# Gate tiles ahead of the waiting tiles in the DeltaNet layer, and row sums written as full 128x128 products

## The chip, the core and the metric

The kernel runs on one core of a Trainium2 chip. A core has TensorE (PE in the profile; its weight loads are listed apart as PEld), VectorE (DVE), ScalarE (ACT), GpSimd (POOL) and SyncE (SP, whose queue issues the transfers here). The metric is the device time of one execution in microseconds; lower is better.

## The reference, cut to what matters

A trunk of four layers over 272 tokens (16 learned meta tokens and 256 real ones) of width 1024. Every layer is a token mixer and then a SwiGLU network of inner width 2816, each on a normalised copy of the residual and added back to it. The mixers are in turn forgetting attention (FoX, 16 heads of 64), gated linear attention (GLA, 4 heads), gated DeltaNet (8 heads of 128) and FoX again.

```python
for i in range(DEPTH):                       # FoX, GLA, DeltaNet, FoX
    h = h + mixer(rmsnorm(h, norm_mix[i]))
    h = h + swiglu(rmsnorm(h, norm_ffn[i]), w_gate_up[i], w_down[i])

def gdn_mixer(h, ...):                       # the DeltaNet layer
    proj = h @ w_in                          # q, k, v, gate: 1024 columns each; a, beta
    qkv = silu(causal_depthwise_conv(qkv, conv_w))
    q = l2norm(q) * 128 ** -0.5;  k = l2norm(k)
    ...                                      # per chunk and head:
    t_mat = I + strict_lower(kb k^T * decay) # unit lower triangular
    u, w = solve(t_mat, [v beta, kb exp(b)])
    v_new = u - w @ state
    o = (q k^T * decay) @ v_new + (q exp(b)) @ state
    o = rmsnorm(o, o_gain) * silu(gate)
    return o @ w_out
```

FoX normalises q and k per head (a sum of squares over 64 channels), GLA and DeltaNet normalise their outputs per head (256 and 128 channels), and DeltaNet's q and k too. These per-head sums of squares are the row sums of this case.

## The kernel before, in words

**Layout.** Activations are kept transposed: 128 channels on the partitions, 272 tokens along the free axis. A "column tile" is 128 output channels of a projection. Each needs eight input blocks, and each block needs three matmuls of 272 columns, since inputs and weights are split in a high and a low part in a one-pass format (`zh`, `zl` with `wh`, `wl`; `Trunk.block`, where `mm` at L403 is the line that all matmuls carry). These are the dense matmuls. Other matmuls keep plain float32 operands; the trace shows two records for each of them.

**Weights.** Each column tile has one weight unit of 128x1024 (`make_unit`): a transfer of 512 KB on SP's queue, a copy `wh` on ACT, a subtraction `wl` on DVE. Units are made in the order of the column tiles, up to two ahead of the one in use, with three buffers each.

**Order.** The program is written out by one generator-driven planner, `Trunk`, which estimates when each engine is free and emits instructions in that order (`turn`, `step`, `Lane.slot`). Column tiles stand in a list `bg`, first in, first out: at most three are open, and if the tile at the head waits for an event that isn't set, none behind it may start (`step`). Everything else (convolutions, Gram products, the inverse, the solves) is a generator that runs when its inputs are estimated to be there. The planner's estimate of the PE clock counts columns weighted by the rows of the moving operand over 128 (`pe`); it has no price for a change of the used part of the array. The lanes of ACT and DVE put the weight split (`wide`) into the first free slot after its inputs.

**DeltaNet.** `GDN_ORDER` lists the column tiles of its input projection: keys `k`, gates `r`, queries `q`, values `v`. Tiles at place `GDN_FREE` = 19 or later that are not gates wait for `in_ev` (in `gdn`, where `self.dense` is called for the list). `in_ev` is set by `inverse()`: the decays (`decay`), the key norms (`k_done`) and the Gram products (`gram`) lead to 24 lower triangular 96-token blocks, whose 16x16 diagonal blocks are inverted together by a chain of 15 steps on DVE, two instructions each. Then `merge` combines the small inverses by small matmuls, `solve(i)` runs for each head, `wrap` and `out_norm` normalise, and the output projection follows (`finish`). Up to six convolution inputs `xc` are held at a time (`GDN_XC`); queries and values that were projected early wait for `in_ev` with their convolution. A finished gate tile needs one DVE product (`sr` from PSUM times the row scale) and one Silu on ACT (`r_done`), and is not needed before `gated(i)`.

**Row sums.** A sum of squares over the channels of a head is a matmul whose stationary operand is a window of a mostly zero strip (`strip1`, `strip2`) with one or two non-zero columns. The window is 8 columns wide, so the stationary operand is 128x8, and the sum lands in row i of an 8-row output. Four or eight heads are accumulated in one bank. The way back, from 8 rows to 128 partitions, is a matmul of a selector (`sel`, `sel2` through `pick`) with a 64-row tile that holds high and low parts (`rows_tile`, `hilo_rows`): 64 rows of contraction. The norm of the residual uses a 128x128 constant `ones` (`norm_end`).

Of the kernel before, what the change touches and what calls it, by code (L numbers as in the profile page):

```python
# [9 lines left out]
F32R = mybir.dt.float32r  # L10
# [6 lines left out]
DM = 1024  # L17
NM = 16
T = 272
# [8 lines left out]
GLA_GROUP = 8  # L28
# [5 lines left out]
GDN_ORDER = (  # L34
    [("k", i) for i in range(8)]
    + [("r", i) for i in range(5)]
    + [(c, i) for i0 in (0, 4) for c in "qv" for i in range(i0, i0 + 4)]
    + [("r", i) for i in range(5, 8)]
)
KEPT = ("_const_", "_z_", "_wraw_", "_wsp_", "_ps_")  # L40

# [97 lines left out]
def shape_consts():  # L139
    c = Cols()  # L140
    c.add("ident", np.eye(128))
    c.add("ones", np.full((128, 128), 1.0 / DM))
    strip = np.zeros((128, 30))
    strip[:64, 14] = 1.0 / 64
    strip[64:, 15] = 1.0 / 64
    c.add("strip2", strip)
    strip = np.zeros((128, 15))
    strip[:, 7] = 1.0
    c.add("strip1", strip)
    c.add("sel", np.tile(np.eye(32, 16), (4, 1)))  # L150
    return c

# [140 lines left out]
class Trunk:  # L293
# [357 lines left out]
    def norm_end(self):  # L651
        yield self.acc
        p = yield from self.bank()
        self.mm(p[:, :T], self.con("ones"), self.acc)
        self.v.tensor_scalar(self.ms, p[:, :T], EPS, None, ALU.add)
        self.free(p)
        yield from self.rsqrt(self.zp, self.rs, self.ms, rest=True)
        self.set(self.rs_ev)
# [41 lines left out]

        return self.sel[rows, h : h + 1].to_broadcast([rows.stop - rows.start, n])

    def rows_tile(self, pool, name, n=T, rows=64, bufs=None):
        st = pool.tile([128, n], F32R, tag=name, name=name, bufs=bufs)[:rows]
        self.v.tensor_scalar(st, self.con_t[:rows, 0:1].to_broadcast([rows, n]), 0.0, None, ALU.mult)
        return st
# [61 lines left out]
    def fox(self, j, lo, gain):  # L768
        v, s, g = self.v, self.s, self.g
# [8 lines left out]
        with ExitStack() as cx:  # L778
            cp = cx.enter_context(self.tc.tile_pool(name="foxc", bufs=1))
# [38 lines left out]
            GP = FOX_GROUP  # L818

            def qk_done(jp, which):  # L820
                grp, i = jp // GP, 2 * (jp % GP) + which

                def f(p):
                    raw = tp.tile([128, T], F32, tag=f"raw{i}", name="raw", bufs=2)
                    s.activation(raw, p[:, :T], AF.Copy)
                    sq = tp.tile([128, T], F32, tag="sq", name="sq", bufs=3)
                    s.activation(sq, p[:, :T], AF.Square)
                    self.free(p)
                    raws[jp, which] = raw
                    yield sq  # L830
                    if i == 0:
                        ssqs[grp] = yield from self.bank()
                    ssq = ssqs[grp]
                    n = 4 * GP
                    self.mm(ssq[:n, :T], self.con("strip2")[:, 14 - 2 * i : 14 + n - 2 * i], sq, i == 0, i == 2 * GP - 1)
                    if i == 2 * GP - 1:
                        mm = tp.tile([n, T], F32, tag="mm", name="mm")
                        v.scalar_tensor_tensor(mm, ms[:n], EPS, ssq[:n, :T], ALU.mult, ALU.add)
                        self.free(ssq)
                        y = tp.tile([n, T], F32, tag="y", name="y")  # L840
                        yield from self.rsqrt(self.zp, y, mm)
                        ys = self.rows_tile(tp, "ys")
                        self.hilo_rows(ys, y, 0)
                        yield ys
                        for i2 in range(2 * GP):
                            jq = grp * GP + i2 // 2
                            p = yield from self.bank()
                            self.mm(p[:, :T], self.sel2[:, i2], ys)
                            r = raws[jq, i2 % 2]
                            v.scalar_tensor_tensor(r, r, kg if i2 % 2 else qg, p[:, :T], ALU.mult, ALU.mult)  # L850
                            self.free(p)
                            if i2 % 2:
                                self.set(qk_ev[jq], r, raws[jq, 0])
                return f
# [124 lines left out]
    def gla(self, j, lo, gain):  # L979
        v, s, g = self.v, self.s, self.g  # L980
# [3 lines left out]
        with ExitStack() as cx:  # L984
# [3 lines left out]
            cp = cx1.enter_context(self.tc.tile_pool(name="glac", bufs=1))  # L988
# [193 lines left out]
            def out(i):  # L1182
                yield at_ev
                yield v_ev[i]
                hd, grp = i // 2, i // GLA_GROUP
                p = yield from self.bank()
                for i3, (t0, n) in enumerate(TILES):
                    self.mm(p[:, t0:T], vsb[i3][:, i], at[i3][:n, hd, : T - t0], i3 == 0, i3 == 2)
                obs[i] = post[0].tile([128, T], F32, tag="ob", name="ob", bufs=KD)
                s.activation(obs[i], p[:, :T], AF.Copy)  # L1190
                self.set(o_ev[i], obs[i])
                yield from self.hold("sq", 3)
                sq = tp.tile([128, T], F32, tag="sq", name="sq", bufs=3)
                s.activation(sq, p[:, :T], AF.Square)
                self.free(p)
                yield sq
                if banks[grp] is None:
                    banks[grp] = yield from self.bank()
                r = hd % (GLA_GROUP // 2)
                self.mm(banks[grp][:8, :T], self.con("strip1")[:, 7 - r : 15 - r], sq, count2[grp] == 0, count2[grp] == GLA_GROUP - 1)  # L1200
                self.drop("sq")
                count2[grp] += 1
                if count2[grp] == GLA_GROUP:
                    self.set(s_ev[grp])
# [42 lines left out]
    def out_norm(self, new, tp, mm, ob, g_ev, oh_ev, tiles, row):  # L1247

        v = self.v
        y = self.zp.tile([128, T], F32, tag="nsq", name="y", bufs=2)[:8]  # L1250
        yield from self.rsqrt(self.zp, y, mm)
        ys = self.rows_tile(self.zp, "nacc", bufs=2)
        self.hilo_rows(ys, y, 0)
        for i in tiles:
            self.oh[i], self.ol[i] = new("oh"), new("ol")
        self.oh_ready = True
        yield ys
        for i in tiles:
            yield g_ev[i]
            p = yield from self.bank()  # L1260
            self.mm(p[:, :T], self.pick(slice(0, 64), row(i)), ys)
            yield from self.hold("vt", 2)
            og = tp.tile([128, T], F32, tag="vt", name="og")
            v.tensor_mul(og, ob[i], p[:, :T])
            self.free(p)
            self.split(self.oh[i], self.ol[i], og)
            self.drop("vt")
            self.set(oh_ev[i], self.oh[i], self.ol[i])


    def gdn(self, j, lo, gain):
        v, s, g = self.v, self.s, self.g
# [4 lines left out]
        with ExitStack() as cx:  # L1277
# [87 lines left out]
            def row_sum(name, i, sq):  # L1365
                if i % 4 == 0:
                    bank[name] = yield from self.bank()
                self.mm(bank[name][:8, :T], self.con("strip1")[:, 7 - i % 4 : 15 - i % 4], sq, i % 4 == 0, i % 4 == 3)
                self.drop("sq")

            def decay():
# [6 lines left out]
                for i0 in range(0, H, GDN_DECAYS):  # L1378
                    ps = yield from self.bankn(GDN_DECAYS)
                    for i, p in enumerate(ps, i0):  # L1380
                        self.mm(p[:96, 0:T], self.pick(slice(0, 64), i, 96), bs, True, False)
                        self.mm(p[:96, T:448], self.pick(slice(0, 64), i, 96), bs[:, 96:], False, False)
                        self.mm(p[:96, 0:96], eye, dmask[:, 0:96], False, False)
                        self.mm(p[:96, T:448], eye, dmask, False, True)
                    for i, p in enumerate(ps, i0):
# [8 lines left out]
            def k_done(i):  # L1394
                def f(p):
# [12 lines left out]
                    if i == 0:  # L1408
                        bank["k"] = yield from self.bank()
                    for i3, (t0, n) in enumerate(TILES):  # L1410
                        self.mm(bank["k"][:n, 8 * i3 + i : 8 * i3 + i + 1], sq[:, t0 : t0 + n], self.con("strip1")[:, 7:8])
                    self.drop("sq")
                    if i == H - 1:
                        pk = bank["k"]
# [304 lines left out]
    def run(self):  # L1719
        nc, tc = self.nc, self.tc  # L1720
        self.new_pools()
        with ExitStack() as cx:
# [6 lines left out]
            self.par_t = cp.tile([128, self.pcols.n], F32, name="par")  # L1729
            self.con_t = cp.tile([128, self.ccols.n], F32, name="con")  # L1730
            self.sel = cp.tile([128, 16], F32R, name="sel")
            self.sel2 = cp.tile([64, 4, 128], F32R, name="sel2")
            self.next_norm()
            self.nblock = 8 * 3
            self.make_unit()
# [10 lines left out]
            def start():  # L1746
                for k in range(KD):
                    self.norm_z(k, f"g_mix{self.layers[0][0]}")
                for k in range(KD):
                    self.norm_sum(k)  # L1750
                self.v.tensor_copy(self.sel, self.con("sel"))
                pairs = self.con("sel")[:64, 0:8].rearrange("p (i a) -> p i a", a=2)
                self.v.tensor_copy(
                    self.sel2.rearrange("p i (a b) -> p i a b", a=2), pairs[:, :, :, None].to_broadcast([64, 4, 2, 64]))
                yield from self.norm_end()

            self.go(start())
# [47 lines left out]
```

## Time and profile before

| | |
|---|---|
| median of three runs | 1587.0 us (1582.32 to 1587.86) |
| profiled execution, its own time | 1581.87 us |
| its span | 1580.1 us |
| mean granted PE clock | 0.977 |
| PE busy | 1518.4 us (96%) |
| DVE busy | 1097.7 us (69%) |
| ACT busy | 779.7 us (49%) |

The span is the traced stretch; 1.8 us of the execution lie around it. PE records overlap, since matmuls are pipelined: the distance between the starts of two matmuls says what one costs, not its listed duration. The granted clock is 1.00 at full speed and 0.50 at half speed; dense matmuls then start about 0.125 or 0.227 us apart.

### The profile page before, as it was taken

The numbers are of one execution on the slowest core, as the hardware profiler recorded it, in microseconds if no ns is written. First come the engines' busy times: TensorE is split into PE (matmuls) and PEld (weight loads), VectorE is DVE, ScalarE is ACT, GpSimd is POOL, SyncE is SP. The second block draws the span as 40 slices with busy tenths as digits, with TensorE's granted clock in tenths as the row PEclk, the third lists the DMA queues.
The fourth block names the chain that finished last, engine by engine and source line by source line (L and its number), as shares of the span: only waits on it lengthen the run. The fifth ranks groups of instructions, "written<-read, shape, count | busy, mean of one in ns | idle before, by whom it ended". The sixth has DMA issues, their size and how long they took to land.

```text
span 1580.1 us, 29533 instructions
## 1 busy us (share of the span) xinstructions
PE 1518.4 (96%) x11985; PEld 1443.8 (91%) x11985; DVE 1097.7 (69%) x2159; ACT 779.7 (49%) x1417; POOL 17.1 (1%) x56
## 2 busy tenths in 40 slices
PE   6999999999999999999895998999999999999999
PEld 6788999999998899999795887999999788999999
DVE  7677676665795776655879467876656777786653
ACT  5456554444445544444564344544444555654442
POOL 0000000000000000000100000000000000000000
PEclk9999999999999999999997899999999999999999
DMA  5232455555423455555332022455555323455564
GB/s 173 94 121 94 149 174 173 174 178 178 154 97 99 141 174 174 174 179 179 98 121 67 15 77 84 147 175 175 174 177 174 106 94 121 134 186 188 187 197 138
DMA packets 63897, 225.80 MB, mean 143 GB/s; under 512 B 7256, under 2 KB 9664, under 8 KB 63760
## 3 DMA queue, kind: packets, MB, share of 16 engines
q1 hardware_dynamic: 63760, 223.91, 43.9%
q8 instruction: 94, 1.54, 0.4%
q14 instruction: 43, 0.35, 0.1%
HBM read 222.83 MB, written 1.05 MB: 142 GB/s over the span
## 4 chain that ended last, share of the span: by engine, by line
PE 82%; DVE 8%; issue 5%; ACT 4%; DMA 1%; SPq 0%; POOL 0%; DVEq 0%; ACTq 0%; POOLq 0%
PE ps L403 81%; DVE wl L244 1%; PE ps L408 1%; ACT wh L244 1%; ACT pr L244 1%; DVE pr L244 1%; DMA w<-in_w_dram 1%; ACT d L244 1%; DVE sm L244 1%; DVE rq L244 1%; DVE tmp L244 0%; DVE ri L244 0%; DVE yc L244 0%; ACT pts L244 0%; DVE gx L244 0%
## 5 line engine op out<-in xcount | busy, mean ns | idle before, releaser
L403 PE MATMUL ps<-zh,wh 128*128 128x272 f32 (+1 forms) x2400 | 710.8, 296 | 12.4 <-ACT zh L244 10.1
L403 PE MATMUL ps<-zh,wl 128*128 128x272 f32 (+1 forms) x2400 | 697.0, 290 | 3.9 <-DVE wl L244 3.9
L403 PE MATMUL ps<-zl,wh 128*128 128x272 f32 (+1 forms) x2400 | 697.1, 290 | 0.0
L244 ACT ACTIVATE wh<-w 128x1024 fp32r<-128x1024 f32 x420 | 443.5, 1056 | 397.4 <-PE ps L403 232.5
L244 DVE TENSOR_TENSOR wl<-w,wh 128x1024 fp32r<-128x1024 f32 x420 | 512.2, 1221 | 166.8 <-ACT wh L244 166.5
L403 PEld LDWEIGHTS ps<-zh,wh 128*128 128x128 f32 x2400 | 458.9, 191 | 35.8 <-issue 17.9
L403 PEld LDWEIGHTS ps<-zh,wl 128*128 128x128 f32 x2400 | 458.9, 191 | 5.5 <-DVE wl L244 5.2
L403 PEld LDWEIGHTS ps<-zl,wh 128*128 128x128 f32 x2400 | 458.9, 191 | 0.3 <-DVE zl L244 0.2
L403 PE MATMUL ps<-al,wh 128*128 128x272 f32 (+1 forms) x704 | 202.0, 287 | 0.0
L403 PE MATMUL ps<-ah,wl 128*128 128x272 f32 (+1 forms) x704 | 201.3, 286 | 0.0
L403 PE MATMUL ps<-ah,wh 128*128 128x272 f32 (+1 forms) x704 | 200.7, 285 | 0.0
L403 PEld LDWEIGHTS ps<-ah,wh 128*128 128x128 f32 x704 | 133.0, 189 | 0.0
L403 PEld LDWEIGHTS ps<-al,wh 128*128 128x128 f32 x704 | 132.4, 188 | 0.0
L403 PEld LDWEIGHTS ps<-ah,wl 128*128 128x128 f32 x704 | 132.2, 188 | 0.0
L244 DVE TENSOR_TENSOR s<-t,rs 128x272 f32<-128x272 f32 (+1 forms) x88 | 38.5, 437 | 64.9 <-ACT t L244 64.7
L244 DVE TENSOR_TENSOR al<-a,ah 128x272 fp32r<-128x272 f32 (+1 forms) x88 | 38.6, 438 | 64.4 <-ACT ah L244 64.3
L403 PE MATMUL ps<-oh,wh 128*128 128x272 f32 (+1 forms) x256 | 75.5, 295 | 1.9 <-ACT wh L244 1.2
L403 PE MATMUL ps<-oh,wl 128*128 128x272 f32 (+1 forms) x256 | 74.9, 293 | 0.9 <-DVE wl L244 0.9
L403 PE MATMUL ps<-ol,wh 128*128 128x272 f32 (+1 forms) x256 | 74.7, 292 | 0.0
L244 ACT ACTIVATE ah<-a 128x272 fp32r<-128x272 f32 (+1 forms) x88 | 36.8, 418 | 62.8 <-DVE a L244 62.8
L244 ACT ACTIVATE zh<-h,par 128x272 fp32r<-128x272 f32 x64 | 32.6, 519 | 69.6 <-DVE h L244 68.9
L244 ACT ACTIVATE t<-t 128x272 f32<-128x272 f32 (+1 forms) x88 | 36.3, 416 | 37.1 <-DVE t L244 37.0
(224 smaller groups left out, 1499.6 us busy)
## 6 DMA issues: line engine op xcount, KB each, us to landing
w<-in_w_dram SPq DMA_DIRECT2D x420, 512.0 KB, 3.3
h<-in_h_dram SPq DMA_DIRECT2D x4, 272.0 KB, 4.9
out_dram<-h SPq DMA_DIRECT2D x8, 128.0 KB, 4.0
rst<-in_rst_dram SPq DMA_DIRECT2D x1, 576.0 KB, 5.4
mask<-in_fmask_dram SPq DMA_DIRECT2D x2, 210.0 KB, 5.4
con<-in_con_dram SPq DMA_DIRECT2D x1, 158.5 KB
mask<-in_gmask_dram SPq DMA_DIRECT2D x1, 126.0 KB, 3.1
par<-in_par_dram SPq DMA_DIRECT2D x1, 87.5 KB, 3.1
```

What stands on the lines that cost most here:

```text
L244: r = f(*args, **kw)
L403: ins = self.nc.tensor.matmul(out, lhsT, rhs, start=start, stop=stop)
L408: ins = self.nc.tensor.transpose(out, in_, self.con("ident")[:n, :n])
```

## The change

Two edits. The first reorders `GDN_ORDER`: the last three gate tiles (r5, r6, r7) stood at the end of the list, behind all queries and values; they now stand after the first four queries and the first two values, at places 19 to 21. The tiles that wait for `in_ev` (v2, v3, q4 to q7, v4 to v7) come behind them, with the same waits. The host packs the weights in the new order, so the transfers are the same ones in another order.

The second widens the operands of the row sums and of the way back. Stationary windows are 128 columns instead of 8 (one strip of 270 columns in place of two, with the same non-zero columns), so the output covers 128 rows, of which the same few are read. The selectors and the tile they multiply have 128 rows instead of 64, the added ones zero. `ones` is one column, broadcast to 128.

```diff
 GDN_ORDER = (
     [("k", i) for i in range(8)]
     + [("r", i) for i in range(5)]
-    + [(c, i) for i0 in (0, 4) for c in "qv" for i in range(i0, i0 + 4)]
+    + [("q", i) for i in range(4)]
+    + [("v", i) for i in range(2)]
     + [("r", i) for i in range(5, 8)]
+    + [("v", i) for i in range(2, 4)]
+    + [(c, i) for c in "qv" for i in range(4, 8)]
 )
...
-    c.add("ones", np.full((128, 128), 1.0 / DM))
-    strip = np.zeros((128, 30))
+    c.add("ones", np.full((128, 1), 1.0 / DM))
+    strip = np.zeros((128, 270))
     strip[:64, 14] = 1.0 / 64
     strip[64:, 15] = 1.0 / 64
-    c.add("strip2", strip)
-    strip = np.zeros((128, 15))
-    strip[:, 7] = 1.0
-    c.add("strip1", strip)
+    strip[:, 142] = 1.0
+    c.add("strip", strip)
...
-        self.mm(p[:, :T], self.con("ones"), self.acc)
+        self.mm(p[:, :T], self.con("ones").to_broadcast([128, 128]), self.acc)
...
-    def rows_tile(self, pool, name, n=T, rows=64, bufs=None):
+    def rows_tile(self, pool, name, n=T, rows=128, bufs=None):
...
-                    self.mm(ssq[:n, :T], self.con("strip2")[:, 14 - 2 * i : 14 + n - 2 * i], sq, i == 0, i == 2 * GP - 1)
+                    self.mm(ssq[:, :T], self.con("strip")[:, 14 - 2 * i : 142 - 2 * i], sq, i == 0, i == 2 * GP - 1)
...
-                self.mm(banks[grp][:8, :T], self.con("strip1")[:, 7 - r : 15 - r], sq, count2[grp] == 0, count2[grp] == GLA_GROUP - 1)
+                self.mm(banks[grp][:, :T], self.con("strip")[:, 142 - r : 270 - r], sq, count2[grp] == 0, count2[grp] == GLA_GROUP - 1)
...
-            self.mm(p[:, :T], self.pick(slice(0, 64), row(i)), ys)
+            self.mm(p[:, :T], self.pick(slice(0, 128), row(i)), ys)
...
-                self.mm(bank[name][:8, :T], self.con("strip1")[:, 7 - i % 4 : 15 - i % 4], sq, i % 4 == 0, i % 4 == 3)
+                self.mm(bank[name][:, :T], self.con("strip")[:, 142 - i % 4 : 270 - i % 4], sq, i % 4 == 0, i % 4 == 3)
...
-                        self.mm(p[:96, 0:T], self.pick(slice(0, 64), i, 96), bs, True, False)
-                        self.mm(p[:96, T:448], self.pick(slice(0, 64), i, 96), bs[:, 96:], False, False)
+                        self.mm(p[:96, 0:T], self.pick(slice(0, 128), i, 96), bs, True, False)
+                        self.mm(p[:96, T:448], self.pick(slice(0, 128), i, 96), bs[:, 96:], False, False)
...
-            self.sel2 = cp.tile([64, 4, 128], F32R, tag="sel2", name="sel2")
+            self.sel2 = cp.tile([128, 4, 128], F32R, tag="sel2", name="sel2")
```

More of the change, by code (lines that the diff above doesn't have):

```diff
@@ L1410, in f @@
                     for i3, (t0, n) in enumerate(TILES):
-                        self.mm(bank["k"][:n, 8 * i3 + i : 8 * i3 + i + 1], sq[:, t0 : t0 + n], self.con("strip1")[:, 7:8])
+                        self.mm(bank["k"][:n, 8 * i3 + i : 8 * i3 + i + 1], sq[:, t0 : t0 + n], self.con("strip")[:, 142:143])
                     self.drop("sq")
@@ L1731, in run @@
             self.sel = cp.tile([128, 16], F32R, name="sel")
-            self.sel2 = cp.tile([64, 4, 128], F32R, name="sel2")
+            self.sel2 = cp.tile([128, 4, 128], F32R, name="sel2")
             self.next_norm()
@@ L1751, in start @@
                 self.v.tensor_copy(self.sel, self.con("sel"))
-                pairs = self.con("sel")[:64, 0:8].rearrange("p (i a) -> p i a", a=2)
+                pairs = self.con("sel")[:, 0:8].rearrange("p (i a) -> p i a", a=2)
                 self.v.tensor_copy(
-                    self.sel2.rearrange("p i (a b) -> p i a b", a=2), pairs[:, :, :, None].to_broadcast([64, 4, 2, 64]))
+                    self.sel2.rearrange("p i (a b) -> p i a b", a=2), pairs[:, :, :, None].to_broadcast([128, 4, 2, 64]))
                 yield from self.norm_end()
```

## The prediction

> **What bounds the kernel now.** I read the page first (totals, the strip of slices, the chain that ended last), then PE's waits, then the order of time around the longest wait and around single row sums.
>
> ```profile
> span 1580.1 us, 29533 instructions
> PE 1518.4 (96%) x11985; PEld 1443.8 (91%) x11985; DVE 1097.7 (69%) x2159; ACT 779.7 (49%) x1417; POOL 17.1 (1%) x56
> PE   6999999999999999999895998999999999999999
> PEclk9999999999999999999997899999999999999999
> PE 82%; DVE 8%; issue 5%; ACT 4%; DMA 1%; SPq 0%; POOL 0%; DVEq 0%; ACTq 0%; POOLq 0%
> PE ps L403 <- DVE xm L244: 15.1, 1, 15.1
> ```
>
> PE is the bound nearly everywhere: 96% busy and 82% of the chain. The exception is one place, slice 21 (830 to 869 us), where PE is half busy and the granted clock dips: PE waits 15.1 us in one piece for `xm`, the small inverses. So PE time saved in the dense stages should come off the span, and work put into that hole is nearly free if it is not missed later.
>
> ```profile
> 843.05 0.29 PE L403 MATMUL ps<-zl,wh 128*128 128x272 f32 x1
> 858.43 1.56 PE L403 MATMUL ps<-xm,l 96*96 96x96 f32 x8 [15.09 <-DVE xm L244]
> 860.75 0.43 PE L403 MATMUL ps<-zh,wl 128*128 128x272 f32 x1
> 860.98 0.43 PE L403 MATMUL ps<-zl,wh 128*128 128x272 f32 x1
> 837.49 0.43 DVE L244 TENSOR_TENSOR xc<-ps,rs 128x272 f32<-128x272 f32 x1
> 837.84 1.21 DVE L244 TENSOR_TENSOR wl<-w,wh 128x1024 fp32r<-128x1024 f32 x1
> 838.97 0.43 DVE L244 TENSOR_TENSOR xc<-ps,rs 128x272 f32<-128x272 f32 x1
> 843.00:859.00 16.00, 0.91 (x7) 0.71 (x6) 14.75 (x32) 3.15 (x5) 0.00 (x0) 0.59 0.15 48
> ```
>
> The last row gives, for 843 to 859, busy time of PE, PEld, DVE, ACT and POOL, the clock and the share of DMA. DVE works 14.75 of the 16 us: it is the bound inside the hole. Behind it dense matmuls start 0.23 us apart (860.75, 860.98: half clock); at full clock it is 0.125 us, as the four equal steps of the last rows of part two show.
>
> **Part one, the gate tiles.** They gain PE cover in the hole. Three tiles are 3 x 8 x 3 = 72 matmuls, at 0.125 us 9.0 us. They may start at 843, since nothing ahead of them in the list waits for `in_ev` any more. They do not fill the hole: 9.0 of 15.1 us.
>
> They also bring DVE work into it. Units are made two tiles ahead, so at 843 the two next units are split already, as v2's and v3's are now; while the three gate tiles run, three more splits `wl` and three scalings `sr` are due. By the DVE rows, start to start, a product costs 837.84 - 837.49 = 0.35 us and a split 838.97 - 837.84 = 1.13 us: together 3 x 1.48 = 4.4 us. They go into the queue between the steps of the inverse (the planner puts a split into the first free slot), so whatever stands behind them, the remaining steps, the transposes and the copies to `xm`, ends 4.4 us later, and `merge` and the waiting tiles with it. Three copies `wh` and three Silu on ACT fall where ACT is busy 3.15 of 16 us: nothing. The three transfers on SP's queue are the same ones in another order; at 15% of DMA they cost nothing.
>
> What was late next? The gates stood behind v7 and covered the last solves. There:
>
> ```profile
> 954.46 0.78 DVE L244 TENSOR_TENSOR xc<-ps,rs 128x272 f32<-128x272 f32 x2
> 960.35 0.42 ACT L244 ACTIVATE vt<-yc 128x272 f32<-128x272 f32 x1
> 966.61 0.49 PE L408 MATMUL ps<-con,vt 128*96 128x128 f32 x3
> 980.97 0.62 PE L403 MATMUL ps<-sq,con 128*8 128x272 f32 x2
> 986.89 0.73 PE L403 MATMUL ps<-nacc,sel 64*128 64x272 f32 x4 [2.83 <-DVE nacc L244]
> L403 PE MATMUL ps<-zh,wh 128*128 128x272 f32 x8 | 2.6, 329 | 0.0
> ```
>
> v7 is projected by 954.5 and its convolved values `vt` are ready at 960.8, but the transpose starts only at 966.61, behind gate blocks on PE: 5.8 us that vanish. The last row is the group of a projection's first matmuls between 966.6 and the last row sum at 980.97: eight more blocks of r6 and r7 stand among the solves, 24 matmuls or 3.0 us. So the stretch from v7 to the output projection shrinks by about 8.8 us, nearly the 9.0 us of work taken out; it is not pure latency. The wait of 2.83 us for the row scale stays. Sum: +4.4 (later inverse) - 8.8 = **-4.4 us**. Bounds: if the tail is pure latency, +4.4; if the splits delay nothing and two half-clock windows after the hole and in the tail go too, -9.0 - 3.4 = -12.4 (a window at half clock is 3.4 us in this trace and costs half of it, 1.7).
>
> **Part two, the row sums.** Here the distances between starts decide. A row sum with the 8-column window, the norm's product (128x128, same two records of 272 columns), and a way back with 64 and one with 128 rows, each between dense matmuls:
>
> ```profile
> 1230.31 0.29 PE L403 MATMUL ps<-zl,wh 128*128 128x272 f32 x1
> 1230.53 0.62 PE L403 MATMUL ps<-sq,con 128*8 128x272 f32 x2
> 1231.08 0.39 PE L403 MATMUL ps<-zh,wh 128*128 128x272 f32 x1
> 1231.31 0.29 PE L403 MATMUL ps<-zh,wl 128*128 128x272 f32 x1
> ...
> 206.14 0.29 PE L403 MATMUL ps<-zl,wh 128*128 128x272 f32 x1
> 206.26 0.62 PE L403 MATMUL ps<-nacc,con 128*128 128x272 f32 x2
> 206.85 0.28 PE L403 MATMUL ps<-zh,wl 128*128 128x272 f32 x1
> ...
> 515.79 0.29 PE L403 MATMUL ps<-zl,wh 128*128 128x272 f32 x1
> 516.01 0.39 PE L403 MATMUL ps<-nacc,sel 64*128 64x272 f32 x1
> 516.56 0.29 PE L403 MATMUL ps<-zh,wl 128*128 128x272 f32 x1
> 815.98 0.29 PE L403 MATMUL ps<-zl,wh 128*128 128x272 f32 x1
> 816.10 0.41 PE L403 MATMUL ps<-brs,sel 128*128 128x272 f32 x2
> 816.48 0.29 PE L403 MATMUL ps<-zh,wl 128*128 128x272 f32 x1
> ```
>
> From the dense matmul before to the second one behind: 1231.31 - 1230.31 = 1.00 us with the narrow window, 206.85 - 206.14 = 0.71 us with the full array. The narrow one loses time on both sides (0.22 us to enter instead of 0.12). So a full-array row sum is 0.29 us cheaper. The way back takes 516.56 - 515.79 = 0.77 us with 64 rows; with 128 rows two take 816.48 - 815.98 = 0.50, four equal steps, so one takes 0.375: 0.39 us cheaper.
>
> ```profile
> L403 PE MATMUL ps<-sq,con 128*8 128x272 f32 x112 | 34.8, 399 | 0.8 <-ACT sq L244 0.8
> L403 PE MATMUL ps<-ys,sel 64*128 64x272 f32 x32 | 6.6, 330 | 6.6 <-DVE ys L244 6.6
> L403 PE MATMUL ps<-nacc,sel 64*128 64x272 f32 x16 | 4.3, 339 | 2.8 <-DVE nacc L244 2.8
> L403 PEld LDWEIGHTS ps<-sq,con 128*8 128x8 f32 x112 | 5.8, 87 | 8.9 <-issue 2.4 <-ACT sq L244 1.2 <-PE ps L403 0.4
> L403 PEld LDWEIGHTS ps<-nacc,con 128*128 128x128 f32 x16 | 2.5, 188 | 0.2 <-DVE nacc L244 0.2
> ```
>
> 112 records are 56 row sums. In the order of time they stand in 52 places, 43 of them between instructions that use the array in full (over 64 rows and columns): 43 x 0.29 = 12.5 us. At the other nine a neighbour is narrow itself, one change remains; I count 0.1 us each, 0.9. The 48 ways back stand in 17 places; three of them sit at a wait for their own input (the 6.6 and 2.8 us of the rows, and one at 958), so 14 x 0.39 = 5.5 us. Together 18.9 us of PE time. The 16 products of the decays, 64 rows too, alternate with full ones, but ACT's exponentials bound that stretch: nothing (up to 2.6 us if not). PE is the bound where these stand, but not in every instant, and DVE and ACT feed the same places; I take 85%: **-16 us**. Bounds: -21.5, all of it with the decays; and the loads below on the other side.
>
> Loads speak against this: 188 ns for 128 columns, 87 for 8. Both 188-ns loads of the norm's product lie inside the 0.71 us, so they hide. [...]
>
> The constants' transfer grows from 158.5 to 207.5 KB. It is issued at 4.12 and first used by DVE at 12.27:
>
> ```profile
> 4.12 0.49 SPq L376 DMA_DIRECT2D con<-in_con_dram  x1
> 12.27 0.17 DVE L244 CAST sel<-con 128x16 fp32r<-128x16 f32 x1
> ```
>
> Eight us of cover for a third more bytes: nothing, and at most 1 us without the cover. DVE's zeroing on 128 rows instead of 64 has the same free size: nothing. `ones` as a broadcast column reads like the selectors of the way back, broadcast already: nothing. The planner counts twice the columns for the way back, which may shift its order elsewhere: 0, within 3 us to either side.
>
> **Sum.** 1581.87 (own time of the profiled execution) - 4.4 - 16.0 = 1561.5. That execution was 5.1 us under the median of the runs shown and at their lowest; I add half of it, 2.5: **1564 us**.
>
> **Rivals.** (a) The tail gives the gates back: solves, `wrap` and scaling are a latency chain that starts 4.4 us later and does not shorten. For it: the 2.83 us wait for the row scale, which no filler can cover. Against: the transpose that stood 5.8 us behind gate blocks. 1581.9 + 4.4 - 16 + 2.5 = 1573. (b) Another engine takes half of part two, since DVE and ACT set the pace in FoX between PE's waits: 1581.9 - 4.4 - 8 + 2.5 = 1572. Against: DVE is 69% busy. (c) Everything counts: -18.9, -9.0 and -3.4: 1553. (d) Slower: the wide loads are exposed, because a row sum's squares arrive just in time and its load cannot be drawn ahead. Place: all 112 records; price between 188 - 87 = 101 ns (11.3 us) and the full 188 ns (21.1 us), say 16.2, in place of the 16 us saved: 1581.9 - 4.4 + 16.2 + 2.5 = 1596. It decides against the change from 4.4 / 112 = 40 ns of exposed load each. Against it: 0.71 us in the norm's place, whose sum also arrives last. (e) The gates do not go into the hole, for want of a bank or a weight buffer, and only part two counts: 1568. Against: three tiles may be open, and the units ahead of 843 are split.
>
> **How the numbers follow.** Forecast 0.54, (a) 0.15, (b) 0.11, (c) 0.10, (d) 0.06, (e) 0.04. A measurement of this kernel tells about 0.5%, 8 us, from no change: faster means under 1579. The forecast's own range is 1556 to 1572; (a), (b) and (e) end at its edge, (c) a little below. The range 1550 to 1577 leaves out (d) and some of the spill of (a) to (c). All cases but (d) are faster; with spill above 1579 from (a) and (b): faster 0.86, within 0.5% 0.08, slower 0.06.
>
> **What would show it.** Right: dense matmuls with `sr` behind them between 843 and 852, the wait for `xm` down from 15.1 to about 10.5 us and ending near 863 (less what part two saves earlier); row-sum places at 0.71 us and ways back at 0.375; the transpose of v7's values right behind `vt`. Wrong: records of row sums with their load ahead of an idle PE (d); waits of PE for `pts`, `ys` or `vt` growing by what the row sums save (b); a longer wait for `nacc` before the output projection of that layer (a).

## The result and the profile after

The changed kernel takes 1559.5 us (median; 1556.54 to 1563.87), the kernel before 1587.4 us beside it (1582.32 to 1588.07; its medians in the later measurements are 1582.4 to 1583.6): a ratio of 0.9833, 95% interval 0.9802 to 0.9865. In a second measurement the ratio was 0.9858 (0.9829 to 0.9887). The prediction was 1564.

The profiled execution took 1560.21 us. Its page, totals, the strip of slices and the chain that ended last:

```profile
span 1558.4 us, 29526 instructions
PE 1498.1 (96%) x11985; PEld 1453.9 (93%) x11985; DVE 1096.2 (70%) x2159; ACT 780.2 (50%) x1417; POOL 17.1 (1%) x56
PE   8899999999999999999897998999999999999999
PEclk9999999999999999999898898999999999999999
PE 78%; DVE 9%; ACT 6%; issue 5%; DMA 0%; SPq 0%; POOL 0%; DVEq 0%; ACTq 0%; POOLq 0%
```

PE's busy time fell by 20.3 us (1518.4 to 1498.1), the span by 21.7. The weight loads grew by 10.1 us (1443.8 to 1453.9), which is about 0.09 us for each of the 112 loads of the row sums; they don't keep the span from shrinking. In the strip, slice 21 (818 to 857 us, the wait for the small inverses) has gone from half busy to seven tenths. PE's waits, as waiter, what it waited for, us in total, times, longest; the row by itself is the wait for `pts` (FoX) in the kernel before:

```profile
PE ps L404 <- DVE xm L245: 11.4, 1, 11.4
...
PE ps L404 <- ACT pts L245: 7.9, 15, 1.3
...
PE ps L404 <- DVE nacc L245: 5.3, 1, 5.3
...
PE ps L404 <- DVE ys L245: 2.7, 1, 2.7
```

```profile
PE ps L403 <- ACT pts L244: 6.7, 12, 1.3
```

Three of them have changed by more than 2 us. The wait for `xm` is 3.7 us shorter, the wait for the row scale before the output projection (`nacc`) 2.5 us longer, and the first wait for `ys`, in the first FoX layer, has shrunk from 6.6 to 2.7 us. The prediction expected the first, put the second under a rival, and did not have the third.

The hole in order of time, PE first, then DVE (start, duration, engine, line, operation, out and in):

```profile
844.09 0.29 PE L404 MATMUL ps<-zl,wh 128*128 128x272 f32 x1
855.82 1.41 PE L404 MATMUL ps<-xm,l 96*96 96x96 f32 x7 [11.44 <-DVE xm L245]
```

```profile
840.25 1.23 DVE L245 TENSOR_TENSOR wl<-w,wh 128x1024 fp32r<-128x1024 f32 x1
...
841.59 0.43 DVE L245 TENSOR_TENSOR sr<-ps,rs 128x272 f32<-128x272 f32 x1
842.53 1.23 DVE L245 TENSOR_TENSOR wl<-w,wh 128x1024 fp32r<-128x1024 f32 x1 [0.51 <-ACT wh L245]
843.67 0.44 DVE L245 TENSOR_TENSOR tmp<-gx,gl 96x162 f32<-96x162 f32 x1
```

PE now has dense work until 844.4, and the splits `wl` and products `sr` of the gate tiles stand on DVE between the steps `tmp` and `gx` of the inverse, as predicted. At 842.53 the split even waits half a microsecond for ACT's copy, with the next step behind it in the queue.

A row sum and a way back, each with the dense matmuls around it:

```profile
1200.16 0.29 PE L404 MATMUL ps<-zl,wh 128*128 128x272 f32 x1
1200.29 0.62 PE L404 MATMUL ps<-sq,con 128*128 128x272 f32 x2
1200.55 0.49 PE L404 MATMUL ps<-zh,wh 128*128 128x272 f32 x1
1200.87 0.28 PE L404 MATMUL ps<-zh,wl 128*128 128x272 f32 x1
...
509.17 0.29 PE L404 MATMUL ps<-zl,wh 128*128 128x272 f32 x1
509.30 0.29 PE L404 MATMUL ps<-nacc,sel 128*128 128x272 f32 x1
...
509.55 0.29 PE L404 MATMUL ps<-zh,wl 128*128 128x272 f32 x1
```

1200.87 - 1200.16 = 0.71 us, and 509.55 - 509.17 = 0.38 us: both as forecast (0.71 and 0.375, from 1.00 and 0.77).

Where the 21.7 us lie: the table has the stretches from one norm product (`nacc,con`) to the next, in the profiled executions, before, after, and for the two kernels that have one part each (below).

| us | before | after | order alone | wide products alone |
|---|---|---|---|---|
| to the first norm product | 16.8 | 19.1 | 17.1 | 19.3 |
| FoX | 189.4 | 182.7 | 189.2 | 179.9 |
| its FFN | 198.7 | 198.7 | 198.7 | 198.7 |
| GLA | 148.1 | 144.4 | 147.7 | 142.9 |
| its FFN | 203.4 | 202.9 | 203.5 | 202.8 |
| delta rule | 258.3 | 247.0 | 263.6 | 252.2 |
| its FFN | 197.8 | 199.0 | 197.8 | 198.2 |
| second FoX | 181.4 | 178.5 | 181.1 | 178.5 |

Half of the gain is in the delta rule, the rest where only the wide products were meant to act. The first row differs from execution to execution (16.7 to 19.6 over all kernels here). The order alone made the delta rule longer: that is the question of the experiments.

### The profile page after: what moved, and what is told of

Same layout as the page of the kernel before. It is cut to its first block, busy times and chain, and to the rows that moved or that the text cites. A ratio compares the mean times of both kernels' runs of the same rounds, so it can differ in the third digit from the quotient of the medians.

```text
span 1558.4 us, 29526 instructions
## 1 busy us (share of the span) xinstructions
PE 1498.1 (96%) x11985; PEld 1453.9 (93%) x11985; DVE 1096.2 (70%) x2159; ACT 780.2 (50%) x1417; POOL 17.1 (1%) x56
## 3 DMA queue, kind: packets, MB, share of 16 engines
HBM read 222.88 MB, written 1.05 MB: 144 GB/s over the span
## 4 chain that ended last, share of the span: by engine, by line
PE 78%; DVE 9%; ACT 6%; issue 5%; DMA 0%; SPq 0%; POOL 0%; DVEq 0%; ACTq 0%; POOLq 0%
PE ps L404 78%; DVE wl L245 2%; ACT pr L245 2%; ACT wh L245 2%; DVE rq L245 1%; DVE pr L245 1%; DVE sm L245 1%; PE ps L409 1%; ACT d L245 1%; ACT pts L245 0%; DVE ri L245 0%; DVE raw L245 0%; DMA h<-in_h_dram 0%; DVE tmp L245 0%; DVE l1p L245 0%
## 5 line engine op out<-in xcount | busy, mean ns | idle before, releaser
L245 ACT ACTIVATE pr<-sm,mn 96x192 f32<-96x192 f32 (+3 forms) x96 | 42.2, 441 | 26.6 <-DVE mn L245 26.5
```

Source lines behind the costliest of these rows:

```text
L245: r = f(*args, **kw)
```

## The experiments

In all of them the lines of the kernel move by a few, so the matmul line is L401 to L406, and that of the added products L408 or L411.

**The two parts, one at a time.** Order alone:

```
-    + [(c, i) for i0 in (0, 4) for c in "qv" for i in range(i0, i0 + 4)]
+    + [("q", i) for i in range(4)]
+    + [("v", i) for i in range(2)]
     + [("r", i) for i in range(5, 8)]
+    + [("v", i) for i in range(2, 4)]
+    + [(c, i) for c in "qv" for i in range(4, 8)]
```

> The order of the column tiles alone; row sums and ways back as before. Theory: the gate tiles fill the hole (wait for xm near 11 us instead of 15.1), the inverse, from its first step to the first merge matmul, lasts 26.6 us instead of 21.2, and the stretch from v7's product with the row scale to the pick of the last scales shrinks by 8 to 10 us. FoX, GLA and the SwiGLU stages stay within 0.5 us. Without anything from the clock the DeltaNet stage (258.3 us between its norm products) becomes 253 us, 5 less, and the time about 0.3% less. Rival 1: the gates give nothing and all of the changed kernel's gain is the arrays': DeltaNet stays at 258. Rival 2: the four half-clock windows between the hole and v7 that the changed kernel no longer had (6.8 us) went because of the new order; then this kernel loses them too and the stage is 246 to 248. If they went because of the wide row sums, they are here still.

Measured: 1587.55 us against 1583.58 before, ratio 1.0030 (1.0015 to 1.0046). The order alone makes the kernel slower, by 4 to 5 us, where it was expected to gain 0.3%.

Wide products alone (the rest of the diff, the list of before):

> Row sums and ways back in the full array, the order of the column tiles as before. Theory: first FoX, GLA and last FoX lose what they lost in the changed kernel (4.4, 3.6 and 2.8 us), the DeltaNet stage 4 to 6 us: 11 row sums and 3 ways back there are 4.4 us by the prices 0.29 and 0.39; the hole stays 15.1 us. In all 15 to 17 us, ratio about 0.990. Rival (the clock): the wide row sums count as more activity and save the half-clock windows after the hole too: DeltaNet loses 10 us or more and the ratio is 0.986. Rival (loads exposed): nothing is gained in FoX and GLA.

Measured: 1559.48 us, ratio 0.9849 (0.9827 to 0.9870). That is -24.1 us, more than the 15 to 17 expected; the delta rule lost 6.1 us of its 258.3, not the 10 of the clock rival. Within the noise the wide products alone give what the whole change gives in its first measurement (0.9833).

**The width of the row sums.** The changed kernel with windows of 64 and of 96 columns in place of 128:

```
-                self.mm(bank[name][:, :T], self.con("strip")[:, 142 - i % 4 : 270 - i % 4], sq, ...)
+                self.mm(bank[name][:64, :T], self.con("strip")[:, 142 - i % 4 : 206 - i % 4], sq, ...)
...                                          # the same for the row sums of FoX and GLA
```

> The changed kernel with windows of 64 columns for the accumulated row sums (the output covers 64 rows), all else as changed. Theory: what costs is the change between a part of the array and the whole of it, so with 64 columns a row sum between dense matmuls takes 1.00 us again, as with 8 columns, and FoX gives back 3 to 4 us in each layer, GLA 2. Rival: the load of the narrow window was the cost, in proportion to something in its width: then 64 columns lie half way, 0.85 us, or are as quick as 128, 0.71 us.

> The changed kernel with windows of 96 columns. Theory: over 64 columns count as the whole array, so a row sum between dense matmuls takes 0.71 us as with 128 columns and FoX and GLA stay as in the changed kernel within 1 us. Rival: every width under 128 is a part of the array: 1.00 us, and FoX gives back 3 to 4 us in each layer.

One execution each: 1564.86 us with 64 columns, 1557.83 with 96; single times that differ by no more than those of one kernel do, so the places decide. A place in order of time, with 64 and then with 96:

```profile
27.63 0.28 PE L404 MATMUL ps<-zl,wh 128*128 128x272 f32 x1
27.84 0.67 PE L404 MATMUL ps<-sq,con 128*64 128x272 f32 x2
28.45 0.39 PE L404 MATMUL ps<-zh,wh 128*128 128x272 f32 x1
28.68 0.29 PE L404 MATMUL ps<-zh,wl 128*128 128x272 f32 x1
```

```profile
29.92 0.29 PE L404 MATMUL ps<-zl,wh 128*128 128x272 f32 x1
30.05 0.62 PE L404 MATMUL ps<-sq,con 128*96 128x272 f32 x2
30.31 0.49 PE L404 MATMUL ps<-zh,wh 128*128 128x272 f32 x1
30.63 0.29 PE L404 MATMUL ps<-zh,wl 128*128 128x272 f32 x1
```

28.68 - 27.63 = 1.05 us with 64 columns, no better than 8 columns (1.00); 30.63 - 29.92 = 0.71 us with 96, as cheap as 128. So the price does not grow with the columns: it is paid at 8 and at 64 columns and not at 96 or 128. A small part lies on the way in (0.21 us to the row sum's start in place of 0.13), the larger on the way back (0.84 us from there to the second dense matmul in place of 0.58). The prices that the traces show are 0.29 us for a row sum of two records and 0.39 us for a way back of one.

**The order again, beside its twin, and the waits filled with work.** By the runs so far the order costs 4 to 5 us alone and is worth near nothing on top of the wide products. One suspect was the clock: the profile of the order alone has stretches at half clock in the delta rule, in which PE is busy for 46.2 us. So the changed kernel and the wide products alone ran side by side, and each again with full-array products of no use in the wait for `xm` and in the wait for the last row scale. Nobody reads their results; everything else is computed as before. Shown is the part in the wait for `xm`:

```
+    def fill(self, p, z, n):
+        for i in range(n):
+            a = (p[:, :T], z[0][i % KD][:, 0:128], z[1][i % KD])
+            ins = self.nc.tensor.matmul(*a, start=True, stop=True)
...
                     yield gx
+                    if i in FILL:
+                        self.fill(fb, z, FILL[i])
...
```

> The changed kernel again, now in the same rounds as its twin without the new order (array2). The order's worth on top of the wide products is after2 minus array2. By the prediction's part one it is -4.4 us (bounds +4.4 and -12.4). By the theory 'the order gains nothing' (the tail keeps most of what the gates took out of it and half-clock windows take the rest) it is within 2 us of zero. Expected: 1559.5, the difference between -2 and +2.

> Wide products and broadcast column alone, the order of before. Expected 1559.5 as in its first look; if part one was worth its -4.4 us, 1564.

> The changed kernel with 111 products of no use (128 x 128 on 272 columns, results read by nobody): 79 in what is left of the wait for xm, 32 in the wait for the last row scale. Every other instruction and its order is that of the changed kernel. Clock theory: the granted clock of a 3.4 us window follows the work PE did in the window before, so the four half-clock windows from 848 and the three from 964 shrink to one or none; gain: about 2 windows of dense or small products behind the hole (3 us) and 967 to 974 at the tail (3 us), sum -5 to -6 us, 1554. Latency theory: what follows both waits hangs on DVE and ACT, PE's clock there costs nothing: 0 to +2 us, 1560 to 1562.

> The same fill in the kernel with wide products alone: 106 such products in the wait for xm, 20 around the wait for the last row scale. Clock theory: the dense matmuls right behind the hole (847.96 to 850.6, 0.23 us apart) go to 0.125, the windows from 834, 855 and 968 go: -5 to -7 us, 1553. Latency theory: 0 to +2. If the order is worth more once the clock is out of it, warm_after ends below warm_array by up to the prediction's 4.4 us; if not, the two agree within 2 us.

Measured, against 1582.44 before: changed kernel 1561.73 (0.9858, 0.9829 to 0.9887), wide products alone 1564.02 (0.9879, 0.9853 to 0.9905), filled 1560.27 (0.9848, 0.9818 to 0.9877) and 1564.02 (0.9886, 0.9861 to 0.9912). On top of the wide products the order is worth about 2 to 3 us by the medians and ratios, and the intervals overlap; between the two filled kernels it is 3.8 us by the medians, and those intervals overlap too.

The fill does nothing for the total, though the mean granted clock of the runs is higher with it (0.987 against 0.981 in the changed kernel, 0.984 against 0.979 with the wide products alone). The tail without and with it:

```profile
967.37 1.24 PE L404 MATMUL ps<-nacc,sel 128*128 128x272 f32 x4 [5.29 <-DVE nacc L245]
...
969.39 0.43 PE L404 MATMUL ps<-oh,wl 128*128 128x272 f32 x1
969.62 0.45 PE L404 MATMUL ps<-ol,wh 128*128 128x272 f32 x1
```

```profile
961.63 3.30 PE L411 MATMUL ps<-zl,zh 128*128 128x272 f32 x25
...
968.35 0.29 PE L405 MATMUL ps<-oh,wh 128*128 128x272 f32 x1
968.48 0.29 PE L405 MATMUL ps<-oh,wl 128*128 128x272 f32 x1
```

Without the fill the output projection starts at half clock (0.23 us apart), with it at full clock (0.125). From the start of the last four ways back to the next norm product this makes 27.4 us into 25.7. Behind the hole it gains nothing: the stretch from the first `xm` product to DVE's last pair of products `xc` (v7's) stays at 89.9 us (89.6 without). With the wide products alone the half-clock windows that began inside the hole at 834 now begin right behind it, at 852, where `merge`'s products of 96 rows and fewer stand; the fill moved them and did not remove them. So the theory that the lost clock in these two waits ate the order's gain falls: 1.7 us at the tail, nothing at the hole.

**The two halves of the wide products, and where the inverse is late.** Each half with the order of before; as a third, the ways back wide with row sums of 64 columns; as a fourth, the changed kernel with the splits made during the inverse on POOL:

```
# rowsum_only: the wide products alone, but
-    def rows_tile(self, pool, name, n=T, rows=128, bufs=None):
+    def rows_tile(self, pool, name, n=T, rows=64, bufs=None):
-            self.mm(p[:, :T], self.pick(slice(0, 128), row(i)), ys)
+            self.mm(p[:, :T], self.pick(slice(0, 64), row(i)), ys)
...
# back_only: the wide products alone, but (back_64: 64 columns)
-                self.mm(bank[name][:, :T], self.con("strip")[:, 142 - i % 4 : 270 - i % 4], sq, ...)
+                self.mm(bank[name][:8, :T], self.con("strip")[:, 142 - i % 4 : 150 - i % 4], sq, ...)
...
# pool_splits: the changed kernel, but
-        self.v.tensor_sub(wl, w, wh)
+        (self.g if self.inv else self.v).tensor_sub(wl, w, wh)
```

> Order of before, ways back (and decays) over 128 rows, row sums as narrow as before (8 or 16 columns). The matrix engine's order is that of the kernel with wide products alone. By part two's terms: 14 x 0.39 = 5.5 us less than before at 85%, -4.7 us. If instead the ways back carried the gain that the terms do not explain, -10 us or more.

> As back_only, but the row sums with 64 columns. A place with 64 columns took 1.05 us in the first look at that width, one with 8 to 16 columns 1.00 and one with 128 0.71: the switch is paid as before. Price theory: as back_only, or slower by up to 43 x 0.05 = 2 us. [...]

> Order of before, row sums over 128 columns, ways back over 64 rows as before. By part two's terms: (12.5 + 0.9) x 85% = -11.4 us. [...] back_only and rowsum_only together should give the wide products' -18 to -24 us.

> The changed kernel, with the splits wl that fall into the inverse made by POOL instead of DVE (six of them). If the three splits and scalings are what makes the small inverses later (26.6 us from the first step to the first xm product, 21.2 in the order of before), the stretch shrinks by about 6 x 1.13 = 6.8 us at most, to 20 to 23 us, and the wait for xm from 11.4 to 5 to 8 us. If the inverse is what the end hangs on, the kernel gains 3 to 6 us (1555); if POOL's splits come late for the gate tiles, PE waits for wl there and the gain is 0.

Measured, against 1582.38 before: ways back 1571.14 (0.9924, 0.9908 to 0.9940), ways back with 64-column row sums 1570.07 (0.9920, 0.9900 to 0.9940), row sums 1570.20 (0.9921, 0.9906 to 0.9936), splits on POOL 1563.56 (0.9890, 0.9855 to 0.9926).

The row sums give -12.2 us where their term was -11.4 (the agreement does not prove the term, as the next rows show). The ways back give -11.2, more than twice their term of -4.7. The two add up to -23.4, the wide products together gave -24.1 and -18.4 in their two measurements. 64 columns in place of 8 change nothing that can be measured (1570.07 against 1571.14).

Most of what the ways back have beyond their term stands in the first FoX layer, at its wait for `ys`. The order alone (as before), ways back alone, row sums alone:

```profile
38.98 1.27 PE L406 MATMUL ps<-ys,sel 64*128 64x272 f32 x4 [5.86 <-DVE ys L247]
```

```profile
40.68 1.27 PE L401 MATMUL ps<-ys,sel 128*128 128x272 f32 x4 [2.53 <-DVE ys L242]
```

```profile
42.02 1.27 PE L401 MATMUL ps<-ys,sel 64*128 64x272 f32 x4 [2.72 <-DVE ys L242]
```

The wait is short in every kernel with the longer tile of constants, whatever its products are, and long in both with the old one. It is the planner: it counts the constants' 49 KB more as 0.14 us, dates everything behind them that much later, and emits another order. In the profiles PE has 168 dense matmuls ahead of this product in the two kernels with the old tile and 192 in every other: one column tile more, which at 0.125 us is 3.0 us of work inside the wait. With nothing but 98 unused columns added to that tile, the program of the kernel before has the first 6547 of its 11254 matmuls in exactly the order of the kernel with ways back alone, and all of them in that of the kernel with row sums alone; its own order departs from that at the 119th. The new order with the same 98 columns has all its matmuls in the order of the changed kernel. These two programs were not run, so their times are not known; what the traces have is the wait (6.6 and 5.9 us against 2.4 to 2.9). One and the same shift, some 4 us, is thus part of both halves: without it the row sums gave about 8 us, less than their term, and the ways back about 7, with whatever the clock adds still in both.

The splits on POOL did not shorten the inverse (26.9 us from its first step to the first `xm` product, 26.6 before that edit; 20 to 23 were expected), and the kernel gained nothing by them. DVE, then POOL, in that kernel:

```profile
825.72 1.56 DVE L245 TENSOR_TENSOR tmp<-gx,gl 96x8 f32<-96x8 f32 x1
...
827.51 0.17 DVE L245 TENSOR_TENSOR tmp<-gx,gl 96x18 f32<-96x18 f32 x1
...
827.92 2.23 DVE L245 TENSOR_TENSOR tmp<-gx,gl 96x32 f32<-96x32 f32 x1
```

```profile
824.86 2.40 POOL L245 TENSOR_TENSOR wl<-w,wh 128x1024 fp32r<-128x1024 f32 x1
827.71 2.39 POOL L245 TENSOR_TENSOR wl<-w,wh 128x1024 fp32r<-128x1024 f32 x1 [0.45 <-ACT wh L245]
```

Products of 96x8 and 96x32 last 0.15 and 0.20 us in the changed kernel; here they last 1.56 and 2.23 us while POOL splits, and end when POOL does (827.28 and 830.15, POOL at 827.26 and 830.10 by start and duration). Between two splits a 96x18 takes its 0.17. These two splits on POOL cost DVE 1.41 and 2.03 us, more than a split of its own (1.13). Whether the inverse would end earlier without the splits is thereby not tested; that they stand between its steps is seen in the rows above.

**What is left of the order alone.** Its rows in the delta rule, and those of kernels that differ from one another in the order. Each row is the stretch from norm to norm: us, busy time of PE, PEld, DVE, ACT and POOL, clock, share of DMA, GB/s. Before; order alone; 64-column row sums with the new order; the same with the old order; the changed kernel; wide products with the old order:

```profile
756.50:1014.80 258.30, 232.28 (x1785) 210.50 (x1785) 188.86 (x414) 129.58 (x290) 2.18 (x25) 0.89 0.26 84
```

```profile
756.30:1020.00 263.70, 235.26 (x1785) 212.44 (x1785) 188.12 (x414) 129.43 (x290) 2.19 (x25) 0.89 0.24 82
```

```profile
744.70:997.50 252.80, 226.49 (x1775) 208.14 (x1775) 187.17 (x414) 130.08 (x290) 2.83 (x26) 0.91 0.25 85
```

```profile
748.20:1006.90 258.70, 230.70 (x1782) 211.97 (x1782) 188.02 (x414) 129.50 (x290) 2.87 (x26) 0.89 0.24 84
```

```profile
747.80:994.80 247.00, 220.68 (x1775) 208.69 (x1775) 187.40 (x414) 130.46 (x290) 2.88 (x26) 0.91 0.27 87
```

```profile
743.70:995.90 252.20, 224.17 (x1782) 212.01 (x1782) 188.23 (x414) 129.73 (x290) 2.80 (x26) 0.90 0.26 86
```

With the longer tile of constants the order gains in this stretch: 252.8 - 258.7 = -5.9 us with row sums of 64 columns (1.05 us a place), and 247.0 - 252.2 = -5.2 with wide ones (0.71 us a place; -6.8 in the second pair of executions, 247.8 and 254.6). With the old tile it loses: 263.7 against 258.3, +5.4. So the width of the row sums does not decide it; what remains different is the planner's order of the solves and merges, and the ways back, which have 64 rows in both kernels with the old tile. One place where the order alone loses time is seen in three windows of it:

```profile
908.20:911.60 3.40, 3.40 (x49) 2.19 (x48) 1.05 (x3) 1.44 (x6) 0.00 (x0) 1.00 0.00 0
911.60:915.00 3.40, 3.40 (x44) 3.08 (x43) 1.25 (x4) 0.55 (x2) 0.00 (x0) 1.00 0.02 5
915.00:928.60 13.60, 13.60 (x83) 12.18 (x83) 4.30 (x9) 4.12 (x11) 0.10 (x1) 0.50 0.10 39
```

The second group of `merge` falls into 908 to 915 as one block of small products (mostly 32 to 80 rows and columns) with four dense matmuls among them, and the four windows behind run at half clock, with dense matmuls 0.23 us apart. PE is busy throughout. The changed kernel has no half-clock window between 875 and 964. A second such stretch, 966 to 973, holds the last solves. But the kernel before has such windows too, two behind its own block at 904 to 911 and one at 962, so only the surplus counts. Summed over the half-clock windows of the whole delta rule, PE is busy for 41.7 us before and 46.2 with the order alone; with wide products alone it is 36.5, and 30.4 in the changed kernel. At half price (dense matmuls start 0.23 us apart there, and 0.125 at full clock) that is +2.2 us of the +5.4, and -3.0 of the -5.2. By this estimate the clock makes up about half of the difference between the two, 5.3 of 10.6 us. That the clock is the cause of that half, and what makes the rest, was not tried: the new order with the unused columns is the kernel that would tell.

## Why the prediction was right, and where it was not

**The hole.** Predicted: the gates stand before it, the wait for `xm` goes from 15.1 to about 10.5 us. Measured 11.4, with the last dense matmul at 844.4 and `sr` and `wl` of the gates on DVE. Right.

**The later inverse.** Predicted +4.4 us, three splits and three products. From its first step to the first `xm` product the stretch is 21.2 us before and with the wide products alone, 26.6 with the order, with or without them: +5.4. The missing microsecond fits the waits of the splits and products themselves (0.31, 0.32 and 0.51 us in DVE's rows, for ACT's copy or PE), which the sum did not have.

**The tail.** Predicted -8.8 from v7 to the output projection. From the start of DVE's products that hold v7's to the start of the last four ways back: 29.4 us with the wide products alone, 21.9 with the order too: -7.5. The transposition of v7's values starts at 951.45, right behind `vt` (950.82 with 0.43 us); the rival's longer wait for `nacc` came as well (2.8 to 5.3), and did not take the gain back. The whole delta rule gets 5.2 to 6.8 us shorter by the order on top of the wide products, and the FFN behind it 0.8 longer. Of the 5.2 us, 3 are fewer windows at half clock by the estimate above, and not the gates' cover. Over the runs, 2 to 3 us are left (3.8 with the waits filled), where the step said 4.4 within +4.4 and -12.4.

One step does not hold, and it is one that the prediction put at nothing: "The planner counts twice the columns for the way back, which may shift its order elsewhere: 0, within 3 us to either side." The shift is there, by another cause than it named (the transfer's size, not the columns), and it is large. It makes the first FoX layer's wait for `ys` 3 to 4 us shorter in every kernel with the wide products. And the part on the order was worked out as if it stood by itself; by itself it costs 4 to 5 us, on the planner's order of before.

**The row sums and ways back.** The prices were right to the hundredth: 0.71 and 0.38 us. Their share that reaches the span was not. The cleanest stretch is the second FoX layer, where the planner's order of matmuls is the same in all kernels, and in these three the clock is full (the ways back alone have two half-clock windows there and take 183.1 us, so their share cannot be read): before, row sums alone, wide products alone:

```profile
1212.60:1394.00 181.40, 176.44 (x1399) 155.10 (x1398) 141.12 (x397) 105.46 (x246) 0.00 (x0) 1.00 0.37 120
```

```profile
1204.00:1383.10 179.10, 172.61 (x1398) 158.95 (x1397) 141.19 (x397) 105.26 (x246) 0.00 (x0) 1.00 0.35 122
```

```profile
1194.10:1372.60 178.50, 171.65 (x1398) 158.91 (x1398) 141.05 (x397) 105.11 (x246) 0.00 (x0) 1.00 0.36 122
```

PE has 4.8 us less to do (176.44 to 171.65) and the stretch is 2.9 us shorter: 60% arrives, where the sum took 85%. The rest is time in which PE now stands idle (5.0 us became 6.9), as rival (b) had it; over the whole execution the wait for `pts` grows from 6.7 to 7.9. The -16 came out nearly whole all the same, because two things filled it up: the planner's shift, and windows at half clock. The mean granted clock over the runs is 0.977 before and 0.980 with the wide products, and a line fitted through the runs of all kernels, each with its own level, falls by 1.2 us per 0.001 of it: some 4 us. That it holds between kernels as well is an assumption, and the filled kernels, whose clock rose inside waits, go against it. A second estimate is lower: PE is busy at half clock for 56 us of the profiled execution before and for 45 to 59, 51 on average, in the two profiles each of the changed kernel and of the wide products alone; half of 5 us is 2.5. The prediction had the clock only in its bounds.

**The exposed loads (rival d).** PEld grew by 10.1 us and the places cost 0.71 us with the loads inside. A load of 128 columns lasts 189 ns here, one of 8 columns lasted 87, so 102 ns less:

```profile
L404 PEld LDWEIGHTS ps<-sq,con 128*128 128x128 f32 x112 | 17.4, 189 | 5.2 <-ACT sq L245 3.7 <-issue 0.8
```

The load is hidden all the same: it lies inside the 0.71 us.

**The constants' transfer.** Eight us of cover held: no wait on it shows. It acted through the planner's estimate instead.

So the forecast of 1564 holds with its signs and most of its terms; inside it, -3.9 of the planner's shift and -2.5 to -4 of the clock by the two estimates, neither of them in the sum, stand in the place of a share that was put too high (60% of 18.9 us is 11, where 16 were taken) and of an order that gave 2 to 3 us and not 4.4. That they made up for it is luck.

## What to carry to other kernels

A row sum of 8 or 64 columns, or a way back of 64 rows, that stood between full matmuls cost 0.3 to 0.4 us more here than one padded with zeros to the full 128 (1.00 and 1.05 against 0.71 us, 0.77 against 0.38; 96 columns did as well, 0.71), and the longer weight load (189 ns against 87) lies inside the lower price. Before the parts of a change are priced, look at what the program's own planner reads (sizes, counts): a tile of constants that grew by 49 KB re-ordered the kernel from its 119th matmul on, and that was worth about 4 us at one wait, as much as some of the parts. And a gain on a bound engine is to be weighed by how much of its saved work reaches the span in a clean stretch, 60% here with PE at 97% of it.

## What the runs showed of the hardware that was not expected

- Row sums with 96 columns cost what 128 cost (0.71 us), with 64 what 8 cost (1.05 and 1.00).
- Two half-clock windows, there in one execution of the changed kernel and not in another, cost less than half of themselves. The first FoX layer with two of them at 158 us and without (same columns as above):

```profile
19.10:201.80 182.70, 173.40 (x1347) 159.80 (x1346) 139.21 (x397) 101.71 (x241) 0.00 (x0) 0.97 0.37 118
```

```profile
18.50:198.40 179.90, 170.36 (x1347) 157.14 (x1346) 139.42 (x398) 101.81 (x242) 0.00 (x0) 0.99 0.38 120
```

  2.8 us for two windows of 3.4 us, 1.4 us each in this pair of executions, where the prediction had 1.7. Windows inside waits cost nothing that shows: in the filled kernels the mean clock of the runs rose from 0.981 to 0.987 and from 0.979 to 0.984, and the time stayed (1561.73 and 1560.27, 1564.02 and 1564.02 us).
- A PE that the profile shows as busy all the time can be at half clock: 13.60 of 13.60 us at 0.50, behind a block of small products. What lowers the clock there was not shown; 64-column row sums in place of 8 changed nothing that can be measured (1570.07 against 1571.14 us).
- While POOL ran a split of 2.4 us, small products `tmp` of the inverse on DVE lasted until it ended (0.15 us became 1.56, 0.20 became 2.23).
